# Three fixed experts in place of two, in a mixture-of-experts stage that streams its weights

## Chip, cores and metric

The kernel runs on one core of one Trainium2 chip. The metric is the device time of one execution in microseconds (us). Three runs of the kernel before gave 758.07, 760.01 and 759.18 us, median 759.18 us.

## What is computed

An encoder trunk of two layers over 256 tokens of 1024 features, all in float32. Layer 0 mixes tokens by gated linear attention, layer 1 by a gated recurrence (RG-LRU). Each mixer is followed by a mixture of 16 experts. The part that matters here:

```python
N_EXPERTS, N_GROUPS, TOP_K, D_EXPERT = 16, 4, 2, 512

def grouped_moe(h, router_w, router_bias, w_gate, w_up, w_down):
    scores = jax.nn.sigmoid(t @ router_w)              # 256 tokens x 16 experts
    ...        # the best of 4 groups of 4 experts, then the best 2 experts in it
    for e in range(N_EXPERTS):
        he = jax.nn.silu(t @ w_gate[e]) * (t @ w_up[e])
        out = out + combine[:, e:e + 1] * (he @ w_down[e])

def setup_inputs(seed=0): ...
```

Each token goes to two experts, so 512 places are dealt out per layer. An expert's weights are 6 MB (gate, up and down, 2 MB each), all experts of a layer 96 MB. How many tokens an expert gets follows from the inputs alone. The reference's router, evaluated over `setup_inputs(0)` (jax with its present default random generator), gives for experts 0 to 15:

| layer | tokens per expert |
|---|---|
| 0 | 19, 32, 31, 40, 49, 25, 75, 33, 6, 7, 2, 11, 44, 13, 46, 79 |
| 1 | 27, 37, 33, 27, 24, 42, 12, 30, 13, 16, 26, 15, 73, 27, 46, 64 |

## The kernel before

All weights go through one ring of 17 tiles of 1 MB (`SLOTS`), in the order of one long list of pieces (`Stream`). SyncE's queue issues every load; `Stream.get` hands out the next piece and issues loads up to `look` pieces ahead. A tile of the ring can be loaded again when the piece, 17 allocations earlier, has been used. Some intermediate tensors (`big`) take tiles of the same ring.

The experts are computed in 7 **units** of 128 token places each (`UNITS`, L28 to L36). An entry `(kind, i, n)` gives `n` times 32 places to one expert: kind `"s"` is the fixed expert number `i`, kind `"r"` is the expert of rank `i` when the other experts are sorted by their token counts, largest first. So in the kernel before experts 0 and 1 are fixed with 64 places each, ranks 0 and 1 of the other fourteen have 96 places each, ranks 2 to 7 have 64, and ranks 8 to 13 have 32. `NS` is the number of fixed experts, `ND = 16 - NS` that of the sorted ones.

`route_order` (L934) works out the sorting on VectorE at the end of the routing, just before the expert stage; SyncE reads an expert's number from its result (`value_load`, L242) before the first load of a sorted expert, as the load's address depends on it. A fixed expert's load has no such wait (`f.known`, L257). `Stream.ahead` stops at the first piece that is not known yet. In `out_route` (L499) and again in `gather_end` (L928), after `route_order`, the stream is told to go 16 pieces ahead; the first unit's 12 pieces are those of the fixed experts. Each unit gathers its tokens, multiplies by gate and up (`up_proj`, L1023, called twice), applies silu and product on ScalarE and VectorE, transposes, multiplies by down, and adds the weighted result into `x` (`scatter`, L1056).

`route_end` (L955) compares each expert's token count with its places (`ce`, 32 times `n`) and sets a flag if any count is larger (L972 to L975). `overflow` (L1063), which is called ahead of the sixth unit in both layers (L1137), reads the flag on the engines and skips its body when it is 0. When it is 1, the body computes, for the tokens that found no place, all 16 experts over all 256 tokens, one expert per turn of a hardware loop:

```python
with tc.If(flag > 0):                      # L1067
    ...
    with tc.For_i(0, NE, 1) as e:          # L1079
        def load(name, n, j, q):
            t = h.rearrange("p m n -> p (m n)")
            nc.sync.dma_start(t, I[name][l][ds(e, 1), q * n:(q + 1) * n, :] ...)
```

Each `load` brings 1 MB into the same tile `h`; there are six per turn (gate, up and down, two halves each), and after each one there are eight 128x512 matmuls that read it (two blocks of 128 tokens times four). Between up and down lie silu, a product, eight transposes and two copies; after the second half of down, four times a `scalar_tensor_tensor` and a `tensor_add` of 128x512 on VectorE.

Of the kernel before, what the change touches and what calls it, by code (L numbers as in the profile page):

```python
# [26 lines left out]

UNITS = [  # L28
    [("s", 0, 2), ("s", 1, 2)],
    [("r", 0, 3), ("r", 8, 1)],  # L30
    [("r", 1, 3), ("r", 9, 1)],
    [("r", 2, 2), ("r", 3, 2)],
    [("r", 4, 2), ("r", 5, 2)],
    [("r", 6, 2), ("r", 7, 2)],
    [("r", 10, 1), ("r", 11, 1), ("r", 12, 1), ("r", 13, 1)],
]  # L36
NS = 2
ND = NE - NS
SLOTS = 17
HALVES = [slice(0, 512), slice(512, 1024)]  # L40
# [35 lines left out]
def trunk(ctx, tc, I, out):  # L76
# [8 lines left out]
    stream = Stream(ring, SLOTS - 4)  # L85

    def bank():
        return pp.tile([P, 512], F32, name="ps")
# [66 lines left out]
    for u, unit in enumerate(UNITS):  # L155
        at = 0
        for kind, i, n in unit:
# [6 lines left out]
            at += n  # L164
    G.iota(rtab[:, 2, :], pattern=[[1, ND]], base=NS, channel_multiplier=0, allow_small_or_imprecise_dtypes=True)

# [58 lines left out]
    def part(t, a, q):  # L225
        sl, at = TAIL[q]
        nc.sync.dma_start(t[:, at:at + 4 * (sl.stop - sl.start)].rearrange("p (j n) -> p j n", j=4),  # L227
                          a[:, :, sl].rearrange("o (p j) n -> (o p) j n", j=4))

    def moe_piece(l, name, kind, i, s, last):  # L230
        src = I[name][l]
        n, j = (512, 4) if name != "moe_w_down" else (256, 2)
        last = last and name == "moe_w_down"

        def f(t):
            if kind == "s":
                assert not last
                a = src[i, s * n:(s + 1) * n, :].rearrange("(p j) n -> p (j n)", j=j)
            else:
                if (l, i) not in regs:  # L240
                    with tc.issue_after(mark["load"]):
                        regs[l, i] = nc.sync.value_load(order[l][0:1, i:i + 1], min_val=NS, max_val=NE - 1)  # L242
                a = src[ds(regs[l, i], 1)]
                if last:

                    late.append((t, a))
                    part(t, a, s)
                    if len(late) == 2 * len(UNITS[-1]):
                        for q in range(2, len(TAIL)):
                            for t, a in late[len(UNITS[-1]):]:  # L250
                                part(t, a, q)
                        late.clear()
                    return
                a = a[:, s * n:(s + 1) * n, :].rearrange("o (p j) n -> (o p) (j n)", j=j)
            b = nc.sync.dma_start(t, a)  # L255
            mark["load"] = b.ins
        f.known = lambda: kind == "s" or order[l] is not None  # L257
        return f

    def moe_pieces(l, unit):  # L260
        return [moe_piece(l, name, kind, i, s, unit is UNITS[-1]) for name in ("moe_w_gate", "moe_w_up", "moe_w_down")
                for s in range(2) for kind, i, n in unit]

# [2 lines left out]
    def plan(l, text):  # L266

        for n in text.split():
            if n[0] == "a":
                stream.add("a", *ada_pieces(l, int(n[1]), int(n[2])))  # L270
            elif n[0] == "A":
                stream.add("a", *ada_pieces(1, int(n[1]), int(n[2])))
            elif n[0] == "i":
                w = (gw_in, lw_in)[l]
                stream.add("i", k_piece(w, 0, int(n[1]) * 512), k_piece(w, 1, int(n[1]) * 512))
            elif n[0] in "IJ":
                stream.add("i", k_piece((gw_in, lw_in)[l], "IJ".index(n[0]), int(n[1]) * 512))
            elif n == "r":
                stream.add("r", gate_piece(I["lru_w_r"][0]), gate_piece(I["lru_w_i"][0]))
            elif n == "o":  # L280
                stream.add("o", *[row_piece(I[("gla_w_out", "lru_w_out")[l]][0], q) for q in range(4)])
            else:
                stream.add("u", *moe_pieces(l, UNITS[int(n[1])]))
# [111 lines left out]
    def rsqrt2(ss):  # L395

        r = sm.tile([P, NM], F32, name="rstd2", bufs=1)
        b = V.scalar_tensor_tensor(r, ss[:, 0], EPS, ss[:, 1], op0=OP.add, op1=OP.add)  # L398
        mark["rsqrt"] = b.ins
        G.tensor_tensor(r, r, half[:, 0:NM], op=OP.pow)  # L400
        return [r[:, m:m + 1] for m in range(NM)]
# [472 lines left out]
    def slots(R, tab, name, ms, first=False):  # L874


        n = len(ms)
        m0 = ms[0]
        pos = R["ps"][:, m0 * NE:(m0 + n) * NE].rearrange("p (m e) -> p m e", m=n)
        ov, sl = rt("ov" + name, n, NE), rt("sl2", NM, NE)[:, 0:n]  # L880
        pw, sv, su = rt("pw2", NM, 2, NE)[:, 0:n], rt("sv" + name, n * 2), rt("su" + name, n * 2, 4)
        V.tensor_tensor(ov, pos, tab[:, 1, None, :].to_broadcast([P, n, NE]), op=OP.is_ge)
        V.tensor_tensor(sl, pos, tab[:, 0, None, :].to_broadcast([P, n, NE]), op=OP.add)
        V.scalar_tensor_tensor(sl, ov, FAR, sl, op0=OP.mult, op1=OP.add)
        V.tensor_tensor(pw, R["oh"][:, m0:m0 + n], sl[:, :, None, :].to_broadcast([P, n, 2, NE]), op=OP.mult)
        V.tensor_reduce(sv, pw.rearrange("p m c e -> p (m c) e"), axis=AX.X, op=OP.add)
        if first:
            return ov, sv, sv[:, :, None]
        V.tensor_tensor(su, sv[:, :, None].to_broadcast([P, 2 * n, 4]), utab[:, None, :].to_broadcast([P, 2 * n, 4]),
                        op=OP.subtract)  # L890
        return ov, sv, su
# [42 lines left out]
    def route_order(l, R):  # L934
# [5 lines left out]
        cmp, prod = [tmp[:, i * 256:i * 256 + ND * ND].rearrange("p (e r) -> p e r", e=ND) for i in range(2)]  # L940
        V.scalar_tensor_tensor(key, cnt[:, NS:], 16.0, desc[:, NS:], op0=OP.mult, op1=OP.add)
        V.tensor_tensor(cmp, key[:, None, :].to_broadcast([P, ND, ND]), key[:, :, None].to_broadcast([P, ND, ND]),
# [12 lines left out]
    def route_end(R, cnt, cmp, prod):  # L955

        for i, dst in ((0, be), (1, ce)):
            V.tensor_mul(prod, cmp, rtab[:, i, None, :].to_broadcast([P, ND, ND]))
            V.tensor_reduce(dst[:, NS:], prod, axis=AX.X, op=OP.add)
        ov, sv, su = slots(R, bc, "", [0, 1])  # L960
# [32 lines left out]
    def moe(l, h, hT, R, gs, g2, done=None):  # L993
# [18 lines left out]
        def groups(unit):  # L1012

            w = min(n for _, _, n in unit)
            w = {1: 1, 2: 2, 4: 4}[w]
            res, at = [], 0
            for i, (_, _, n) in enumerate(unit):
                for q in range(0, n, w):
                    res.append((i, (at + q) * 32, w * 32))
                at += n  # L1020
            return res

        def up_proj(unit, xg, t0):  # L1023
            ps = bank()
            for s in range(2):
                w = [stream.get("u").rearrange("p (j n) -> p j n", j=4) for _ in unit]
                for j in range(4):
                    k = 4 * s + j
                    for i, p0, n in groups(unit):
                        T.matmul(ps[p0:p0 + n], xg[:, k, t0 + p0:t0 + p0 + n], w[i][:, j, :], start=k == 0, stop=k == 7)  # L1030
            return ps
# [99 lines left out]
        for u, unit in enumerate(UNITS):  # L1131
            y = mid("y")
            t0 = (u - 1) % 2 * P if u else 0
            if u == len(UNITS) - 2:
                scatter(*pend)
                pend = None
                overflow()  # L1137
            pg = up_proj(unit, xg, t0)
            if u:
                settle()  # L1140
            pu = up_proj(unit, xg, t0)
            if u == 0:
                spread(R)
# [11 lines left out]
            j = 4 if last else 2  # L1155
# [7 lines left out]
            if last:  # L1163
                for q, (sl, _) in enumerate(TAIL):
                    if q < 2:
                        w = [stream.get("u") for _ in unit]
# [23 lines left out]
    h, hT, R = out_route(0, oT, g1, gf, rest)  # L1190
    ss0 = sm.tile([P, 3, NM], F32, name="ss3", bufs=1)
    moe(0, h, hT, R, gf, g2, done=lambda q: last_squares(q, ss0))
    stream.look = SLOTS - 4
    h, hT = norm(rsqrt2(ss0), gn)
# [16 lines left out]
    def done(q):  # L1211
        last_squares(q, ss)
        for m in range(NM):
            sl = TAIL[q][0]
            V.tensor_mul(o[m][:, sl], x[:, m, sl], fg[0][:, sl])  # L1215

    moe(1, h, hT, R, gf, g2, done)
    r = rsqrt2(ss)
    with tc.issue_after(mark["rsqrt"]):
# [29 lines left out]
```

## Time and profile before

| what | value |
|---|---|
| median of the three runs | 759.18 us |
| the profiled execution's own time | 757.96 us |
| its span, first to last instruction | 756.2 us |
| TensorE busy | 699.6 us, 93% |
| VectorE busy | 340.4 us, 45% |
| ScalarE busy | 131.4 us, 17% |
| bytes moved, mean rate over the span | 286.27 MB, 379 GB/s |

The profile has a page with the busy time of each engine and the span in 40 slices of 18.9 us; and views of the trace: groups of instructions by line, the busy time in chosen stretches, who waited for whom, the chain of waits that ended last, the instructions in order of time, and all instructions of one line. PE is TensorE's matmuls, PEld its weight loads, DVE VectorE, ACT ScalarE, SPq SyncE's queue. A matmul that is pipelined behind another starts before that one has ended, so the time per matmul in a run of them is the busy time of the group over its count, and less than the mean duration. The granted clock is that of TensorE as a share of 2.4 GHz.

### The profile page before, as it was taken

The page shows a single profiled execution, that of the slowest core. Times are in us where ns is not written, and L with a number is a line of the kernel's source. Part 1 is how long each engine was busy: PE and PEld are TensorE (multiplying, and loading weights), DVE is VectorE, ACT ScalarE, POOL GpSimd, SP SyncE. Part 2 cuts the span into 40 slices and gives each one's busy share as a digit, 9 for nine tenths or more (in the row PEclk, how much of TensorE's full clock was granted, in tenths as well). Part 3 has the DMA queues.
Part 4 walks back from the last instruction along what each step waited for, and adds up shares of the span by engine and source line. Part 5 has one row for each costly group of instructions (what it writes and reads, how often), then busy time and mean ns, then how long its engine had stood idle before and what let it go on. Part 6 is the DMA issues. An engine that isn't in the chain of part 4 may idle for free. (4 is left out here: it accounts for less than half of the span.)

```text
span 756.2 us, 9538 instructions
## 1 busy us (share of the span) xinstructions
PE 699.6 (93%) x3559; PEld 342.8 (45%) x3559; DVE 340.4 (45%) x780; ACT 131.4 (17%) x257; POOL 27.4 (4%) x69
## 2 busy tenths in 40 slices
PE   4899899999999999999887999998999999999874
PEld 3345745454633533533226888655433433433212
DVE  3626983897413223231023589996523143140214
ACT  5006112122200000000013166123210010010002
POOL 5000001000000000000000014000000000000000
PEclk9999999999999999999999999999999999999998
DMA  9999999779999999999999999991999999999994
GB/s 304 384 386 387 386 396 386 269 318 384 423 370 422 421 421 420 423 409 422 411 363 379 381 367 350 406 377 59 423 421 419 419 421 421 421 420 410 422 373 150
DMA packets 80445, 286.27 MB, mean 379 GB/s; under 512 B 5991, under 2 KB 16280, under 8 KB 57866
## 3 DMA queue, kind: packets, MB, share of 16 engines
q1 hardware_dynamic: 78752, 284.71, 96.0%
q10 hardware_dynamic: 1258, 0.66, 0.3%
q8 instruction: 30, 0.49, 0.3%
q0 software_dynamic: 384, 0.23, 0.1%
q14 instruction: 21, 0.17, 0.1%
HBM read 284.54 MB, written 1.05 MB: 378 GB/s over the span
## 5 line engine op out<-in xcount | busy, mean ns | idle before, releaser
L1030 PE MATMUL ps<-w 128*32 128x512 f32 (+1 forms) x1280 | 204.1, 593 | 9.6 <-DMA w<-in_moe_w_up_dram 7.4
L1030 PEld LDWEIGHTS ps<-w 128*32 128x32 f32 (+1 forms) x1280 | 61.8, 121 | 148.7 <-issue 121.7
L1041 PE MATMUL ps<-w,s 128*32 128x512 f32 (+1 forms) x512 | 85.0, 594 | 2.7 <-ACT s L1160 2.7
L1147 DVE TENSOR_TENSOR s<-s,ps 128x512 f32<-128x512 f32 x14 | 9.6, 688 | 149.6 <-PE ps L1030 149.6
L1061 DVE TENSOR_TENSOR x<-x,ps 128x512 f32<-128x512 f32 (+1 forms) x60 | 39.1, 652 | 59.7 <-PE ps L1060 59.7
L317 DVE SCALAR_TENSOR_TENSOR acc<-w,cond,acc 128x512 f32<-128x512 f32 x84 | 64.8, 794 | 1.1
L473 PE MATMUL ps<-w 128*128 128x512 f32 x128 | 59.3, 599 | 0.0
L1060 PE MATMUL ps<-mid,s 128*128 128x512 f32 (+1 forms) x120 | 55.1, 581 | 2.9 <-DVE mid L1168 2.6
L740 PE MATMUL ps<-hT,w 128*128 128x256 f32 x256 | 55.7, 379 | 0.0
L1041 PEld LDWEIGHTS ps<-w,s 128*32 128x32 f32 (+1 forms) x512 | 25.6, 123 | 58.3 <-issue 50.9
L740 PEld LDWEIGHTS ps<-hT,w 128*128 128x128 f32 x256 | 48.7, 191 | 6.7 <-ACT hT L423 0.2
L1179 DVE TENSOR_TENSOR mid<-ps,gate 128x512 f32<-128x512 f32 x24 | 16.6, 692 | 64.7 <-PE ps L1041 64.7
L561 PE MATMUL ps<-w,hT 128*128 128x512 f32 x96 | 42.5, 596 | 1.8 <-DVE hT L425 1.0
L904 PE MATMUL ps<-onehot,h 128*128 128x256 f32 x192 | 42.4, 379 | 0.0
L317 DVE SCALAR_TENSOR_TENSOR gate<-w,cond,gate 128x512 f32<-128x512 f32 x56 | 40.9, 748 | 0.9
L1146 ACT ACTIVATE s<-ps 128x512 f32<-128x512 f32 x14 | 8.4, 597 | 183.6 <-PE ps L1030 183.6
L904 PEld LDWEIGHTS ps<-onehot,h 128*128 128x128 f32 x192 | 36.4, 190 | 7.0 <-issue 2.4
L1060 PEld LDWEIGHTS ps<-mid,s 128*128 128x128 f32 x120 | 20.5, 190 | 30.8 <-issue 20.1
L1160 ACT COPY s<-ps 128x512 f32<-128x512 f32 x14 | 8.2, 586 | 147.2 <-PE ps L1158 147.2
L529 PE MATMUL ps<-w,hT 128*128 128x512 f32 x64 | 29.6, 619 | 3.7 <-DVE w L637 3.7
L473 PEld LDWEIGHTS ps<-w 128*128 128x128 f32 x128 | 22.8, 191 | 20.7 <-issue 18.9
L561 PEld LDWEIGHTS ps<-w,hT 128*128 128x128 f32 x96 | 17.8, 190 | 23.9 <-issue 21.0
(261 smaller groups left out, 602.5 us busy)
## 6 DMA issues: line engine op xcount, KB each, us to landing
w<-in_moe_w_gate_dram SPq DMA_DIRECT2D x64, 1024.0 KB, 11.2
w<-in_moe_w_up_dram SPq DMA_DIRECT2D x64, 1024.0 KB, 15.7
w<-in_moe_w_down_dram SPq DMA_DIRECT2D x56, 1024.0 KB, 17.8
w<-in_ada_w_dram SPq DMA_DIRECT2D x48, 1024.0 KB, 13.5
w<-in_gla_w_in_dram SPq DMA_DIRECT2D x12, 1024.0 KB, 14.6
w<-in_moe_w_down_dram SPq DMA_DIRECT2D x16, 512.0 KB, 9.5
w<-in_lru_w_in_dram SPq DMA_DIRECT2D x8, 1024.0 KB, 12.5
w<-in_gla_w_out_dram SPq DMA_DIRECT2D x4, 1024.0 KB, 12.5
```

Of the source, the lines that this page charges most:

```text
L317: V.scalar_tensor_tensor(acc, w, cond[:, k:k + 1], acc, op0=OP.mult, op1=OP.add)
L473: T.matmul(ps, yT[:, k, m * P:(m + 1) * P], w[k // 2][:, k % 2, sl], start=k == 0, stop=k == 7)
L529: T.matmul(ps, hT[:, k, m * P:(m + 1) * P], w[k // 4][:, k % 4, :], start=k == 0, stop=k == 7)
L561: T.matmul(pst[i][m], hT[:, 4 * b + j, m * P:(m + 1) * P], w[:, j], start=b == 0 and j == 0, stop=b == 1 and j == 3)
L740: T.matmul(ps[:, 0:S], w[k // 4][:, k % 4, ct * P:(ct + 1) * P], hT[:, k, :], start=k == 0, stop=k == 7)
L904: T.matmul(ps[j // 2][:, j % 2 * 2 * P:(j % 2 + 1) * 2 * P], hv[:, b, j, :], oh, start=m == 0 and j % 2 == 0, stop=m == 1 and j % 2 == 1, ...
L1030: T.matmul(ps[p0:p0 + n], xg[:, k, t0 + p0:t0 + p0 + n], w[i][:, j, :], start=k == 0, stop=k == 7)
L1041: T.matmul(ps[hf][p0:p0 + n], aT[:, k, p0:p0 + n], w[i][:, j, hf * 512:(hf + 1) * 512], start=k == 0, stop=k == 3)
L1060: T.matmul(ps, wt[:, m * P:(m + 1) * P], y[:, sl], start=True, stop=True)
L1061: V.tensor_add(x[:, m, sl], x[:, m, sl], ps)
L1147: V.tensor_mul(act, act, pu)
L1179: V.tensor_mul(y[:, sl], py[hf], g2[:, sl])
```

## The change

Expert 2 becomes a third fixed expert, with 64 places in the second unit, beside rank 1, which has 64 places there. Rank 0 and rank 8 make the third unit. The thirteen sorted experts have 96 places (rank 0), 64 (ranks 1 to 7) and 32 (ranks 8 to 12). For the second unit the list of pieces has expert 2's four gate and up pieces first, then the other expert's four, then the down pieces in turn; `up_proj` takes the first four pieces together and holds them for its two calls.

```diff
 UNITS = [
     [("s", 0, 2), ("s", 1, 2)],
+    [("s", 2, 2), ("r", 1, 2)],
     [("r", 0, 3), ("r", 8, 1)],
-    [("r", 1, 3), ("r", 9, 1)],
     [("r", 2, 2), ("r", 3, 2)],
     [("r", 4, 2), ("r", 5, 2)],
     [("r", 6, 2), ("r", 7, 2)],
-    [("r", 10, 1), ("r", 11, 1), ("r", 12, 1), ("r", 13, 1)],
+    [("r", 9, 1), ("r", 10, 1), ("r", 11, 1), ("r", 12, 1)],
 ]
-NS = 2
+NS = 3
...
     def moe_pieces(l, unit):
+        if unit is UNITS[1]:
+
+            return [moe_piece(l, name, kind, i, s, False) for kind, i, n in unit for name in ("moe_w_gate", "moe_w_up")
+                    for s in range(2)] + [moe_piece(l, "moe_w_down", kind, i, s, False) for s in range(2) for kind, i, n in unit]
         return [moe_piece(l, name, kind, i, s, unit is UNITS[-1]) for name in ("moe_w_gate", "moe_w_up", "moe_w_down")
                 for s in range(2) for kind, i, n in unit]
...
+        held = []
+
         def up_proj(unit, xg, t0):
             ps = bank()
+            if unit is UNITS[1] and not held:
+                look, stream.look = stream.look, stream.look - 4
+                held.extend(stream.get("u") for _ in range(4))
+                stream.look = look
             for s in range(2):
-                w = [stream.get("u").rearrange("p (j n) -> p j n", j=4) for _ in unit]
+                w = [(held.pop(0) if held and i == 0 else stream.get("u")).rearrange("p (j n) -> p j n", j=4)
+                     for i in range(len(unit))]
```

## Rows read from the trace of the kernel before

**Rows 1.** The page: TensorE's share, and GB/s in 40 slices of the span

```profile
PE 699.6 (93%) x3559; PEld 342.8 (45%) x3559; DVE 340.4 (45%) x780; ACT 131.4 (17%) x257; POOL 27.4 (4%) x69
GB/s 304 384 386 387 386 396 386 269 318 384 423 370 422 421 421 420 423 409 422 411 363 379 381 367 350 406 377 59 423 421 419 419 421 421 421 420 410 422 373 150
```

**Rows 2.** Stretches (us): length, busy time of PE, PEld, DVE, ACT, POOL, clock, DMA share, GB/s

```profile
515.00:520.00 5.00, 3.74 (x19) 2.27 (x19) 3.74 (x12) 1.61 (x4) 0.55 (x1) 1.00 0.01 3
...
525.00:530.00 5.00, 5.00 (x30) 2.86 (x30) 3.43 (x12) 2.79 (x7) 0.00 (x0) 1.00 0.28 79
530.00:535.00 5.00, 5.00 (x26) 1.64 (x24) 4.83 (x28) 1.19 (x1) 0.00 (x0) 1.00 1.01 423
160.00:170.00 10.00, 9.99 (x52) 5.13 (x50) 9.09 (x34) 2.40 (x6) 0.17 (x1) 1.00 0.90 370
170.00:180.00 10.00, 8.19 (x64) 5.67 (x64) 7.33 (x37) 2.47 (x4) 0.40 (x1) 1.00 0.92 378
```

**Rows 3.** Waits of SyncE's queue, first of 150:185, then of 500:530 (total, times, longest)

```profile
SPq L242 <- DVE r_ordi L951: 10.1, 1, 10.1
...
SPq L242 <- DVE r_ordi L951: 17.6, 1, 17.6
```

**Rows 4.** All instructions of L1067 in 315:345 (the skipped branch, layer 0), three rows

```profile
L1067 PEldq COMPARE_BRANCH  x1: 352/352/352, 328.9 to 328.9; - x1
L1067 DVEq EVENT_SEMAPHORE  x1: 21/21/21, 332.2 to 332.2; - x1
  PE ps L1030: 1.3, 1
```

**Rows 5.** TensorE in order of time around that branch (start, us, what)

```profile
327.19 3.70 PE L1060 MATMUL ps<-mid,s 128*128 128x512 f32 x8
332.23 13.95 PE L1030 MATMUL ps<-w 128*64 128x512 f32 x64 [1.33 <-DVEq L1067]
```

**Rows 6.** SyncE's queue in order of time, unit 0 and later, layer 1

```profile
527.42 2.69 SPq L255 DMA_DIRECT2D w<-in_moe_w_gate_dram  x4
531.83 4.34 SPq L255 DMA_DIRECT2D w<-in_moe_w_up_dram  x4
```

**Rows 7.** Groups by line and shape: count, busy us, mean ns, idle before

```profile
L473 PE MATMUL ps<-w 128*128 128x512 f32 x128 | 59.3, 599 | 0.0
...
L317 DVE SCALAR_TENSOR_TENSOR gate<-w,cond,gate 128x512 f32<-128x512 f32 x56 | 40.9, 748 | 0.9
...
L476 DVE TENSOR_TENSOR x<-x,s 128x512 f32<-128x512 f32 x8 | 5.5, 689 | 0.1
```

**Rows 8.** DMA issue to landing: x (512 KB each, L104), then L255 in 527:529

```profile
DMA to landing us min/median/max: 3.7/4.2/4.8
...
L255 SPq DMA_DIRECT2D w<-in_moe_w_gate_dram x2: 343/346/348, 527.4 to 528.6; - x2
...
DMA to landing us min/median/max: 6.1/6.1/6.1
```

**Rows 9.** Chain that ended last: a matmul's end and the load that it let start

```profile
677.10 14.00 PE ps L1030 x64
691.65 19.83 DMA w<-in_moe_w_up_dram
...
715.14 1.07 PE ps L1060 x2
717.40 15.24 DMA w<-in_moe_w_down_dram
```

**Rows 10.** Stretches with a fall of TensorE's clock (columns as in rows 2)

```profile
91.00:94.00 3.00, 0.09 (x2) 0.00 (x0) 2.55 (x17) 0.00 (x0) 0.00 (x0) 1.00 1.05 386
...
95.00:97.00 2.00, 2.00 (x3) 0.97 (x4) 2.00 (x7) 0.00 (x0) 0.00 (x0) 0.50 1.05 387
...
733.00:736.00 3.00, 3.00 (x16) 0.64 (x12) 0.00 (x0) 0.00 (x0) 0.00 (x0) 0.50 1.10 349
736.00:737.00 1.00, 1.00 (x13) 0.33 (x6) 0.00 (x0) 0.00 (x0) 0.00 (x0) 0.91 1.17 362
```

## The prediction made before the change was run

> **What bounds the kernel now.** I read the rate of the DMA engines over the span first, then the stretches where it falls, then who waits there. The reader is to see two things in the 40 slices [rows 1]: the stream runs at about 420 GB/s through both expert stages, and falls to 59 GB/s in one slice, with smaller dips in layer 0. The stretches show that slice from near: from 515 to 529 us nothing moves [rows 2]. SyncE's waits name the reason: for 17.6 us it waits for the expert order, the last product of the routing, before it may load the first sorted expert; in layer 0 it waits 10.1 us, but there earlier loads are still in flight, at 370 to 378 GB/s [rows 2, 3]. TensorE is busy 93% [rows 1], so the two are near balance, and what the stream gains here is paid out only where TensorE later waits for weights.
>
> **What the change saves.** Expert 2's four gate and up pieces need no order. In layer 1 they can be loaded inside the hole: one piece of 1.05 MB at 423 GB/s is 2.48 us, four are 9.9 us [rows 2]. Not all of it stays. Before, the order's arrival let four pieces go at once, at 527.4 us, and the fifth at 531.8, when unit 0's first pieces had been used [rows 6]. After the change those four tiles are filled already, so the first sorted piece goes at 531.8 too, 4.4 us later than now. Net 9.9 - 4.4 = 5.5 us, between 0 (TensorE takes over as the bound) and 9.9. In layer 0 the dips are shallow: 0.12 and 0.10 of two 10 us stretches below 421 GB/s, 2.2 us [rows 2]; I take 2, between 0 and 4. Sum: -7.5 us.
>
> **What it adds beside that.** `held` keeps two up pieces in the ring while gate runs, so tiles come free half a unit later, once per layer; a pause in SyncE's issuing there is covered by the pieces already queued ahead of it. That unit's matmuls become pairs of 64 columns, as unit 0's, in place of fours of 32; the bytes stay, and so do the pieces. The sort shrinks from 14 to 13. All of these I cost at nothing; without the queued pieces, the pause would be up to one gate phase, half of the 13.95 us that a unit's gate and up take [rows 5].
>
> **The places.** The step that decides comes from the reference, not from the trace. Rank 1 had 96 places and gets 64. In layer 0 the largest counts are 79 (expert 15) and 75 (expert 6), neither of them fixed. So rank 1 is expert 6, with 75 tokens: 75 <= 96 before, 75 > 64 after. `route_end` sets the flag and `overflow` runs its body in layer 0, all 16 experts over all tokens, for 11 places. The nearest decision between two groups there has a margin of 0.001 in the scores, so rounding does not move 11 tokens. In layer 1 rank 0 has 73 (<= 96) and rank 1 exactly 64, which is not more than 64; ranks 2 to 7 have at most 46 and rank 8 has 24: no flag there. In the trace of before the branch is skipped [rows 4, 5], as it should be with 79 and 75 places under 96.
>
> **What a turn of that loop costs.** The trace of before does not show one, so each part goes by the nearest rows.
> - Wait for a load. All six loads of a turn go into one tile, so none starts before the last matmul on the one before has ended. From that end to the issue: 691.10 to 691.65, 0.55 us, and 716.21 to 717.40, 1.2 us [rows 9]; I take 0.6, the simpler load. From issue to landing with nothing in front: 3.7 us for 512 KB [rows 8], and 1.24 more for the other half at 423 GB/s, 4.9. The other row agrees: of two pieces issued at 527.4 and 528.6 the second landed 6.1 after its issue, so one alone at about 4.8 [rows 8]. Together 5.5 us, between 5.35 and 7.3 (1.2 + 6.1).
> - Matmuls. Eight at 59.3 / 128 = 0.46 us [rows 7] are 3.7 us at the high clock, 7.4 at half. After an idle stretch of 3 us the clock was at 0.50 although matmuls ran densely, in one place for over 2 us, in another through 733 to 736 and most of the way to 737 [rows 10]. Here every burst follows 5.5 idle us. I take 3.5 us at half clock, which does 1.75 us of the work, and 1.95 us at full: 5.45 us.
> - One piece 10.95 us, six 65.7. Silu, product and transposes lie inside the wait for the first down piece.
> - End of a turn. VectorE's four pairs take 4 x (0.75 + 0.69) = 5.8 us [rows 7]; they can start after two of the last eight matmuls, 1.85 us into the burst, so 2.2 us stick out.
> - Jump back. The nearest row is the skipped branch, for which TensorE stood 1.3 us [rows 4, 5]. I take 1.5, between 0.6 and 4.
> - Sum 65.7 + 2.2 + 1.5 = 69.4 us; 16 turns 1110 us. Way in and out (16 transposes, as many small copies, a few small operations) 8 us.
>
> The loads that are queued when the loop begins hold up its first load, and give the same time back afterwards, as they need not be waited for: zero.
>
> The Trainium skill (Runtime: NRT & Kernel Launch, Instruction fetch mechanics) says that a taken branch whose target isn't in the window already fetched must wait for that code; by it, the jumps would cost a fetch each, and no row here prices one inside a loop. The skipped branch is such a jump, over a long body, and the trace gives it 1.3 us; by the page the sum could only rise.
>
> **The sum.** Against the profiled execution: 757.96 - 7.5 + 1110 + 8 = 1868 us. That execution is 1.2 us under the median of 759.18, nothing beside this.
>
> **The rivals.**
> - *The flag stays 0, and the kernel is faster.* The mechanism is the filled hole alone: 757.96 - 7.5 = 750 us, from 745 to 757. It decides as soon as rank 1 has at most 64 tokens in both layers, which needs other inputs than the ones I counted; with jax's older random generator the two largest counts of layer 0 would be 65 and 52. For it: the hole of 14 us is real [rows 2]. Against: the reference's own seed is 0, and 75 is far from 64.
> - *The clock stays low through the loop.* 6 x (5.5 + 7.4) + 1.4 + 1.5 = 80.3 us a turn, 757.96 - 7.5 + 1285 + 8 = 2043 us. For it: half of each turn is idle. Against: it came back within about 4 us of dense work wherever it fell [rows 10]. The Trainium skill (TensorE: Matmul & The Clock Gate, HAM oscillation) tells of a kernel in which each wait for a load put the whole next burst into the slow clock; by that this rival would be the forecast, but its bursts were shorter than these, and the rows here show the return.
> - *The clock stays high.* 6 x (5.5 + 3.7) + 3.0 + 1.5 = 59.7 us a turn, 1714 us. Against: each wait is longer than the idle stretch that lowered it [rows 10].
> - *Layer 1 overflows too.* If one more token goes to its rank 1, 65 > 64, the loop runs twice: 1868 + 1118 = 2986 us. The nearest second-against-third choice there has a margin of 0.0002, so rounding is unlikely to do it.
>
> **How the numbers follow.** Forecast 0.55, low clock 0.15, high clock 0.10, flag stays 0 0.13, both layers 0.03, something else 0.04. The predicted time is 1868 us. The range runs from the high clock less the lower ends of wait and jump (1714 - 14 - 14, and some 45 for an end of turn that is hidden) to the low clock with 40 for the jump and half of the wait's upper end (2043 + 40 + 86): 1640 to 2160, which leaves out about 0.2. About 0.3%, 2.3 us, is what a measurement can tell from no change: slower 0.87; of the flag's 0.13, faster 0.11 and within that bound 0.02.
>
> **What would show it.** Right: in the trace after, 768 more matmuls of 128x512 (48 a turn) in one stretch that starts near 330 us and takes some 1100, all at the lines of `overflow`; six 1 MB loads per turn, each some 11 us after the one before; a DMA rate of about 91 GB/s there (six pieces, 6.3 MB, in 69 us); the clock falling in each wait; and no such stretch in layer 1. The hole at 515 to 529 us of before, now some 1100 us later, is shorter by about 10 us. Wrong: no matmul at these lines. If they are there and a turn is far from 69 us, the wait for a load and the clock are the terms to look at.

## The result, and the profile after

The changed kernel takes 2124.76 us (2121.73 to 2126.46, three runs) against 759.18 before: 2.798 times as long, 95% interval 2.792 to 2.804. The flag is set in layer 0, the slow path runs there once, and the steps of the prediction's argument can be looked up in the trace.

From the page of the changed kernel: TensorE's busy time, the granted clock in tenths and the rate in 40 slices, now of 53 us each.

```profile
PE 1573.5 (74%) x5047; PEld 710.5 (33%) x5047; DVE 461.1 (22%) x971; ACT 171.9 (8%) x327; POOL 27.4 (1%) x71
...
PEclk9999998888888888888888888888888899999999
...
GB/s 356 387 323 388 418 421 209 59 79 79 79 59 79 79 69 69 79 79 72 66 79 79 59 79 79 72 68 78 79 76 62 79 352 373 366 325 389 421 414 311
```

[Rows 1] showed one hole in the rate. Here the rate lies at 59 to 79 GB/s from the eighth slice to the thirty-second: 25 slices, some 1330 us, in layer 0. The clock is down in these slices and in the one before them, in which the loop begins. Layer 1 has no such stretch.

Groups of instructions by line (count, busy us, mean ns, idle before and what ended it): the matmuls of the slow path, and VectorE's operations at the end of its turns.

```profile
L1107 PE MATMUL ps<-h,hT 128*128 128x512 f32 x1024 | 571.8, 722 | 358.2 <-DMA h<-in_moe_w_gate_dram 203.2 <-DMA h<-in_moe_w_up_dram 155.1
L1129 PE MATMUL ps<-h,mid 128*128 128x512 f32 x512 | 282.1, 714 | 130.4 <-DMA h<-in_moe_w_down_dram 130.4
...
L1135 DVE SCALAR_TENSOR_TENSOR mid<-ps,o_cc,gate 128x512 f32<-128x512 f32 x64 | 48.0, 751 | 355.1 <-PE ps L1129 355.1
...
L1136 DVE TENSOR_TENSOR x<-x,mid 128x512 f32<-128x512 f32 x64 | 44.3, 692 | 2.2
```

Two things are to be seen. TensorE stands 358.2 + 130.4 = 488.6 us until one of 96 loads has landed, 5.1 us each. And there are 1024 + 512 = 1536 matmuls of 128x512, 16 for each load, where the prediction had counted 768: in float32 each matmul of the code is two instructions in this trace.

The place of [rows 5] in the changed kernel, TensorE in order of time (two stretches): the last work ahead of the flag, the first of the slow path, and the sixth unit behind it.

```profile
327.77 3.70 PE L1071 MATMUL ps<-mid,s 128*128 128x512 f32 x8
331.30 1.91 PE L437 MATMUL ps<-ident,h 128*128 128x128 f32 x16
...
1703.51 13.95 PE L1041 MATMUL ps<-w 128*64 128x512 f32 x64 [2.08 <-DVE x L1136]
```

The sixth unit starts at 1703.51 in place of 332.23, 1371.3 us later, and that is the whole of the loss: the spans differ by 2123.0 - 756.2 = 1366.8.

One turn of the loop in order of time (start, us, engine, line, what), from the last burst of the turn before.

```profile
668.36 8.83 PE L1129 MATMUL ps<-h,mid 128*128 128x512 f32 x16 [4.77 <-DMA h<-in_moe_w_down_dram]
...
678.01 0.69 DVE L1136 TENSOR_TENSOR x<-x,mid 128x512 f32<-128x512 f32 x1
680.05 0.17 DVE L1098 COPY o_cc<-o_co 128x2 f32 x1 [1.35 <-PEq L1090]
680.08 14.46 SPq L1093 DMA_DIRECT2D h<-in_moe_w_gate_dram  x2
684.95 9.22 PE L1107 MATMUL ps<-h,hT 128*128 128x512 f32 x16 [7.77 <-DMA h<-in_moe_w_gate_dram]
698.98 8.83 PE L1107 MATMUL ps<-h,hT 128*128 128x512 f32 x16 [4.81 <-DMA h<-in_moe_w_gate_dram]
...
712.59 8.83 PE L1107 MATMUL ps<-h,hT 128*128 128x512 f32 x16 [4.78 <-DMA h<-in_moe_w_up_dram]
726.24 8.83 PE L1107 MATMUL ps<-h,hT 128*128 128x512 f32 x16 [4.82 <-DMA h<-in_moe_w_up_dram]
...
739.95 8.80 PE L1129 MATMUL ps<-h,mid 128*128 128x512 f32 x16 [3.28 <-DMA h<-in_moe_w_down_dram]
753.58 8.83 PE L1129 MATMUL ps<-h,mid 128*128 128x512 f32 x16 [4.83 <-DMA h<-in_moe_w_down_dram]
```

Burst, wait, burst, wait: each load is issued when the burst before it has ended, and each burst begins when its load has landed. The next turn's first load is issued at 765.30, so a turn is 765.30 - 680.08 = 85.2 us, and 16 turns are 1363.5.

From issue to landing of the six loads of a turn (L1093), first over all 96, then for the loop's first load alone, which is issued at 333.2 us while the stream's queued loads still move 421 GB/s (333 to 336 us):

```profile
DMA to landing us min/median/max: 4.7/4.8/8.4
...
DMA to landing us min/median/max: 8.4/8.4/8.4
```

The stretches inside two bursts (length, busy PE, PEld, DVE, ACT, POOL, clock, DMA share, GB/s), which answer to [rows 10]:

```profile
685.00:688.00 3.00, 3.00 (x4) 1.44 (x5) 0.00 (x0) 0.00 (x0) 0.00 (x0) 0.50 0.00 0
688.00:689.00 1.00, 1.00 (x2) 0.34 (x1) 0.00 (x0) 0.00 (x0) 0.00 (x0) 0.50 0.00 0
689.00:694.00 5.00, 5.00 (x12) 1.90 (x10) 0.00 (x0) 0.00 (x0) 0.00 (x0) 0.98 0.00 0
694.00:699.00 5.00, 0.19 (x2) 0.02 (x1) 0.00 (x0) 0.00 (x0) 0.00 (x0) 1.00 0.59 210
699.00:699.50 0.50, 0.50 (x1) 0.28 (x2) 0.00 (x0) 0.00 (x0) 0.00 (x0) 0.95 0.00 0
699.50:702.50 3.00, 3.00 (x5) 1.33 (x4) 0.00 (x0) 0.00 (x0) 0.00 (x0) 0.50 0.00 0
...
703.00:708.00 5.00, 4.81 (x12) 1.83 (x10) 0.00 (x0) 0.75 (x2) 0.00 (x0) 1.00 0.00 0
```

Each burst runs for a while at half clock, although its matmuls follow each other without a gap, and then at full: in the first, four matmuls start in 3 us at 0.50, twelve in 5 us at 0.98. The first burst of a turn, behind 7.77 idle us, is at half clock from its start. The second, behind 4.81, is not: the granted clock is 1.00 all through the wait (694 to 699) and falls only some 0.5 us after the burst has begun. It is low for 3.4 us then. The other four bursts of the turn show the same.

### The profile page after: what moved, and what is told of

Read it like the earlier page. It is cut to its first block, busy times and chain, and to the rows that moved or that the text cites. A ratio compares the mean times of both kernels' runs of the same rounds, so it can differ in the third digit from the quotient of the medians.

```text
span 2123.0 us, 14216 instructions
## 1 busy us (share of the span) xinstructions
PE 1573.5 (74%) x5047; PEld 710.5 (33%) x5047; DVE 461.1 (22%) x971; ACT 171.9 (8%) x327; POOL 27.4 (1%) x71
## 5 line engine op out<-in xcount | busy, mean ns | idle before, releaser
L1107 PE MATMUL ps<-h,hT 128*128 128x512 f32 x1024 | 571.8, 722 | 358.2 <-DMA h<-in_moe_w_gate_dram 203.2
L1107 PEld LDWEIGHTS ps<-h,hT 128*128 128x128 f32 x1024 | 230.8, 231 | 698.7 <-issue 426.7
L1129 PE MATMUL ps<-h,mid 128*128 128x512 f32 x512 | 282.1, 714 | 130.4 <-DMA h<-in_moe_w_down_dram 130.4
L1129 PEld LDWEIGHTS ps<-h,mid 128*128 128x128 f32 x512 | 113.6, 227 | 288.7 <-issue 198.3
L1041 PE MATMUL ps<-w 128*64 128x512 f32 (+1 forms) x1152 | 203.7, 600 | 7.7 <-DMA w<-in_moe_w_up_dram 4.8
L1135 DVE SCALAR_TENSOR_TENSOR mid<-ps,o_cc,gate 128x512 f32<-128x512 f32 x64 | 48.0, 751 | 355.1 <-PE ps L1129 355.1
L1041 PEld LDWEIGHTS ps<-w 128*64 128x64 f32 (+1 forms) x1152 | 63.6, 126 | 144.5 <-issue 123.2
L1052 PE MATMUL ps<-w,s 128*64 128x512 f32 (+1 forms) x448 | 85.0, 595 | 2.7 <-ACT s L1171 2.7
L1136 DVE TENSOR_TENSOR x<-x,mid 128x512 f32<-128x512 f32 x64 | 44.3, 692 | 2.2
L565 PE MATMUL ps<-w,hT 128*128 128x512 f32 x96 | 42.5, 596 | 1.9 <-DVE hT L429 1.0
```

Of the source, the lines that this page charges most:

```text
L565: T.matmul(pst[i][m], hT[:, 4 * b + j, m * P:(m + 1) * P], w[:, j], start=b == 0 and j == 0, stop=b == 1 and j == 3)
L1052: T.matmul(ps[hf][p0:p0 + n], aT[:, k, p0:p0 + n], w[i][:, j, hf * 512:(hf + 1) * 512], start=k == 0, stop=k == 3)
L1107: T.matmul(pm[m], hT[:, k, m * P:(m + 1) * P], w[:, j], start=k == 0, stop=k == 7)
L1129: T.matmul(py[m][hf], aTs[m][:, k], w[:, j, hf * 512:(hf + 1) * 512], start=k == 0, stop=k == 3)
L1135: V.scalar_tensor_tensor(tmp, py[m][hf], cc[:, m:m + 1], g2[:, sl], op0=OP.mult, op1=OP.mult)
L1136: V.tensor_add(x[:, m, sl], x[:, m, sl], tmp)
```

## The experiments

**The places alone, in the kernel before.** Two fixed experts, the old order of the stream, rank 1 with 64 places:

```diff
-    [("r", 1, 3), ("r", 9, 1)],
+    [("r", 1, 2), ("r", 9, 2)],
```

> The kernel before with two fixed experts and its own order of the stream; only rank 1's places go from 96 to 64 (rank 9 gets the 32). Theory (the places set the flag in layer 0, 75 > 64): the loop of 16 turns runs, some 85 us each, 759 + 1367 = about 2125 us, within 10. Rival (the time comes from the third fixed expert or the new order of its pieces): no loop, 759 us.

Measured: 2124.92 us, the changed kernel's time, with the same 1024 and 512 matmuls in the slow path. The loss is in the places. The third fixed expert and the order of its pieces have no part in it.

**The change with places enough.** Ranks 0 and 1 keep 96 places each:

```diff
-    [("s", 2, 2), ("r", 1, 2)],
-    [("r", 0, 3), ("r", 8, 1)],
-    [("r", 2, 2), ("r", 3, 2)],
-    [("r", 4, 2), ("r", 5, 2)],
-    [("r", 6, 2), ("r", 7, 2)],
+    [("s", 2, 2), ("r", 2, 2)],
+    [("r", 0, 3), ("r", 7, 1)],
+    [("r", 1, 3), ("r", 8, 1)],
+    [("r", 3, 2), ("r", 4, 2)],
+    [("r", 5, 2), ("r", 6, 2)],
```

> The changed kernel with its third fixed expert and its order of pieces, but ranks 0 and 1 with 96 places each, ranks 2 to 6 with 64 and ranks 7 to 12 with 32, so that 79, 75 and 73, 64 fit. Theory: no loop in either layer, and the early load of expert 2's pieces is all that is left. By the trace of the changed kernel, where the expert stage of layer 1 ended 1.8 us nearer to its start than before and layer 0 no earlier up to the flag: 755 to 758 us. By the prediction's own term for it: 751 us. Rival (the loss is in the order of the pieces): over 762 us.

Measured: 757.99 us beside 759.65 of the kernel before on that chip, ratio 0.9976 (0.9966 to 0.9987). Run again later: 758.16 beside 759.05, 0.9979 (0.9966 to 0.9991). No loop, and a gain of 0.2%, within the 0.3% that the prediction set as a bound; not the 7.5 us of the prediction's term.

**Half the turns.** `For_i(0, NE, 1)` becomes `For_i(0, 8, 1)` in the changed kernel.

> The changed kernel with 8 turns of the loop in place of 16, so experts 8 to 15 are left out of the slow path (part of the computation is left out). Theory (the time is the number of turns times 85.2 us, way in and out near zero): 2124.8 - 8 x 85.2 = 1443 us. Rival (a large fixed cost of the branch or of its code): clearly more than 1443 us.

Measured: 1442.32 us. Eight turns are 682.4 us, 85.3 each; nothing is left for a large fixed cost of the branch.

**Half the matmuls per load.** In the loop of the changed kernel `for m in range(NM)` becomes `for m in range(1)` for both groups of matmuls, and the second block of 128 tokens shares the first block's matmul results. So its tokens get the expert outputs of other tokens.

> The changed kernel with the loop's matmuls for one block of 128 tokens in place of two, so the second block of the slow path is not computed (part of the computation is left out): 8 matmul instructions read each load in place of 16; loads, VectorE and ScalarE as they are. Theory (the prediction's matmul term was half of what it is, as each matmul of the code is two instructions in float32): a burst of 8 x 0.43 + 1.75 for the half clock at its start = 5.2 us, a turn 6 x (4.8 + 5.2) + 2.9 = 62.9 us, 2124.8 - 16 x 22.3 = 1768 us. Rival 1 (shorter bursts stay at half clock to their end): 6.9 us a burst, a turn 73 us, 1930 us. Rival 2 (the length of a burst does not hang on the number of matmuls): 2125 us.

Measured: 2943.31 us, which none of the three foresaw. The loop runs in both layers here. The second block's wrong values change layer 0's output for the 11 tokens without a place (they all lie in that block), and so layer 1's counts: the reference's router, given layer 0's output with this error, sends 66 tokens to expert 15 in place of 64. That is over the limit. Per turn the run still answers. In order of time, around the end of one turn:

```profile
667.14 5.40 PE L1129 MATMUL ps<-h,mid 128*128 128x512 f32 x8 [4.80 <-DMA h<-in_moe_w_down_dram]
...
677.71 11.56 SPq L1093 DMA_DIRECT2D h<-in_moe_w_gate_dram  x2
682.57 6.33 PE L1107 MATMUL ps<-h,hT 128*128 128x512 f32 x8 [10.03 <-DMA h<-in_moe_w_gate_dram]
```

Eight instructions take 5.40 us in most bursts, against 5.2 expected and 8.83 for sixteen; the wait stays at 4.8 to 5.0. So the length of a burst hangs on the number of instructions, and the clock comes back inside this shorter burst too (at half clock to its end it would be 6.9, as the first rival had it). A turn is (2943.3 - 758) / 32 = 68.3 us, not 62.9. Some 2.3 us of that are VectorE's eight operations, which now outlast the burst: from the last burst's end at 672.5 to the next load at 677.7 it is 5.2 us in place of 2.9. Another 2.6 are the bursts, as the first two of a turn take 6.33 and 5.86 us.

**Loads beside matmuls.** The six loads of a turn go in turn into `h` and one tile of the ring:

```diff
+                two, turn = [h.rearrange("p m n -> p (m n)"), big("two")], []
...
-                        t = h.rearrange("p m n -> p (m n)")
+                        t = two[len(turn) % 2]
+                        turn.append(q)
```

> The changed kernel with the loop's six loads going in turn into two tiles, so a load runs while the matmuls of the one before run. Theory (each turn holds six waits of 4.8 us for a load, and each of them costs 1.75 us more by the clock at the start of the burst behind it): one wait and one fall of the clock a turn are left, 4.8 + 6 x 6.9 + 1.75 + 1.5 for the step between up and down + 2.9 = 52.3 us a turn, 2124.8 - 16 x 32.9 = 1598 us, and a clock near 1.0 in most of the loop. Rival (the loads are not what the loop waits for, or the clock stays low): above 1800 us.

Measured: 1604.16 us, and a turn of 52.3 us by its loads. In order of time:

```profile
659.11 8.59 PE L1109 MATMUL ps<-h,hT 128*128 128x512 f32 x16 [7.81 <-DMA h<-in_moe_w_gate_dram]
667.53 7.03 PE L1109 MATMUL ps<-w,hT 128*128 128x512 f32 x16
...
674.40 7.03 PE L1109 MATMUL ps<-h,hT 128*128 128x512 f32 x16
```

Only the first burst of a turn waits for a load and runs slow at first; the others find theirs landed and take 7.03 us, sixteen instructions 0.43 us apart. Five waits and five falls of the clock, 5 x (4.8 + 1.8), are 33 us a turn: what the loop pays for its single tile.

**Where the gain of the early load goes.** First a miss:

> As e2_places96, but expert 2's pieces wait for the order as a sorted expert's do, so nothing is loaded early; its place in the units and in the list of pieces stays. If the early load is worth 2 to 4 us: 758 to 760 us, e2_places96 faster by that. If the gain of e2_places96 is from the shape of the units or the smaller sort: the same time as e2_places96.

Measured: 757.89 us. It tells nothing of the early load: marking expert 2's pieces as not known moved no wait into SyncE's queue, and its trace has them issued at 511 to 518 us, ahead of the order. So the next kernel makes SyncE read the order before the first of them:

```diff
+                if i == 2 and (l, 2) not in regs:
+                    with tc.issue_after(mark["load"]):
+                        regs[l, 2] = nc.sync.value_load(order[l][0:1, 2:3], min_val=NS, max_val=NE - 1)
```

> As e2_places96, but SyncE reads the expert order before it issues expert 2's first piece, so that none of its pieces is loaded early. (In e3_no_early the wait was not there: the pieces went out ahead of the order all the same, and its time is that of e2_places96.) If the early load is what makes e2_places96 1.7 us faster than the kernel before: the hole in the stream of layer 1 is back, and the time is that of the kernel before, 759.5 us, within 1. If the gain is from the shape of the units or the sort: 758 us as e2_places96.

Measured: 757.92 us, beside 758.16 of the kernel with the early load on the same chip. With or without it, the time is the same. Stretches of 10 us in layer 1 (columns as above), first with the early load:

```profile
510.00:520.00 10.00, 8.74 (x42) 5.36 (x41) 5.91 (x29) 2.71 (x7) 0.55 (x1) 1.00 0.95 400
520.00:530.00 10.00, 8.60 (x52) 5.68 (x53) 7.22 (x38) 4.23 (x9) 0.00 (x0) 1.00 0.30 122
530.00:540.00 10.00, 10.00 (x50) 3.41 (x48) 5.91 (x31) 1.83 (x2) 0.00 (x0) 1.00 0.71 276
540.00:550.00 10.00, 10.00 (x44) 6.68 (x40) 3.77 (x8) 2.30 (x4) 0.00 (x0) 1.00 1.01 423
550.00:560.00 10.00, 9.32 (x47) 3.90 (x47) 3.76 (x9) 1.05 (x2) 0.00 (x0) 1.00 0.65 251
```

and without it:

```profile
510.00:520.00 10.00, 8.74 (x45) 5.69 (x44) 5.80 (x25) 2.85 (x7) 0.55 (x1) 1.00 0.23 93
520.00:530.00 10.00, 8.61 (x49) 5.27 (x49) 7.15 (x38) 4.23 (x9) 0.00 (x0) 1.00 0.24 79
530.00:540.00 10.00, 10.00 (x48) 3.30 (x46) 5.30 (x28) 1.16 (x2) 0.00 (x0) 1.00 1.01 425
540.00:550.00 10.00, 10.00 (x44) 7.13 (x41) 4.44 (x10) 2.30 (x4) 0.00 (x0) 1.00 1.02 422
550.00:560.00 10.00, 9.32 (x46) 3.47 (x46) 3.76 (x9) 1.05 (x2) 0.00 (x0) 1.00 1.01 422
```

The hole is filled at 510 to 520; at 520 to 530 it stays, and two others open, at 530 to 540 and at 550 to 560. Over 500 to 570 us the two kernels miss nearly the same: 17.0 us of streaming at 421 GB/s with the early load, 17.8 without. SyncE's waits in 500 to 560, of the kernel with the early load, name what stands there:

```profile
SPq L255 <- PE ps L1052: 13.6, 2, 11.9
```

It waits 11.9 us for unit 0's first down matmul to free a tile. Without the early load it waits as long, and it issues the pieces behind expert 2's at nearly the same times. SyncE's queue with the early load, then without:

```profile
538.74 4.37 SPq L255 DMA_DIRECT2D w<-in_moe_w_down_dram  x4
555.79 4.72 SPq L255 DMA_DIRECT2D w<-in_moe_w_gate_dram  x4
...
538.06 4.37 SPq L258 DMA_DIRECT2D w<-in_moe_w_down_dram  x4
555.11 4.34 SPq L258 DMA_DIRECT2D w<-in_moe_w_gate_dram  x4
```

Without the early load the DMA engines have a row of pieces still to move during that wait (422 GB/s at 550 to 560). With it they run out of them (251): the ring is full, and nothing is left to load. That can be tried: let unit 0 use its down pieces sooner, by putting its gather for the next two units behind them.

```diff
-            if u % 2 == 0 and u + 1 < len(UNITS):
+            if u and u % 2 == 0 and u + 1 < len(UNITS):
                 xg = prepare(u // 2, R["su"])
...
             py = down_proj(unit, aT)
+            if u == 0:
+                xg = prepare(0, R["su"])
```

> As e2_places96, but in the first unit of each layer the gather for the next two units comes after the down matmuls in place of before them. Theory (with the early load the ring is full and the stream stands at 550 to 555 us in layer 1 until the first down pieces are used): the down pieces are used some 7 us earlier, that second hole shrinks, and up to 3 us are gained at the end: 755 to 757.5 us. Rival (the expert stage waits for the gather, or the silu chain is no longer covered): 759 us or more.

Measured: 754.0 us, ratio 0.9919 (0.9899 to 0.9939); run again, 753.53 us, 0.9922 (0.9901 to 0.9942). This is the version that beats both kernels. The same stretches:

```profile
530.00:540.00 10.00, 10.00 (x48) 3.30 (x46) 4.53 (x26) 0.60 (x1) 0.00 (x0) 1.00 0.88 340
540.00:550.00 10.00, 9.30 (x42) 3.52 (x40) 1.99 (x4) 1.66 (x3) 0.00 (x0) 1.00 1.01 421
550.00:560.00 10.00, 8.58 (x40) 6.28 (x38) 2.87 (x7) 1.26 (x3) 0.00 (x0) 1.00 1.01 423
560.00:570.00 10.00, 10.00 (x48) 3.36 (x48) 3.48 (x8) 0.92 (x2) 0.00 (x0) 1.00 0.76 305
```

The hole at 550 to 560 is gone, a smaller one comes after it, and over 500 to 570 us the stream misses 14.8 us. From 570 to 700 us it runs without a hole in all of these kernels (389 GB/s or more in every 10 us), and what is missed before that is not made up there. Whether the new order alone does it was tried twice, in the kernel before and in the kernel whose pieces wait for the order.

> The kernel before, with two fixed experts, and the first unit's gather for the next two units put after its down matmuls, as in e8_down_first. Theory (e8_down_first is faster because the early load no longer runs into a full ring; without an early load the stream is busy from 529 us on whatever the gather does): the time of the kernel before, 759, within 1 us. Rival (the order of gather and down matmuls alone is worth the 4 to 5 us): 755 us.

Measured: 758.24 us, ratio 0.9985 (0.9972 to 0.9997): a gain of about 1 us, and not the 4 to 5 of the rival.

> e8_down_first with expert 2's pieces waiting for the order, so without the early load. Theory: 758 us, as e7_wait_order; the 4 us of e8_down_first need the early load and the order of the gather together. Rival (the order alone): 754 us as e8_down_first.

Measured: 756.79 us, ratio 0.9967 (0.9955 to 0.9979), about 1 us under the 758 expected; the interval overlaps that of the same kernel with the gather first (0.9967 to 0.9999). Over 500 to 570 us its stream misses 17.9 us, 3.1 more than with the early load. With the third fixed expert the four kernels make a table, in us:

| | gather first | down first |
|---|---|---|
| pieces wait for the order | 757.9 | 756.8 |
| pieces loaded early | 758.0 to 758.2 | 753.5 to 754.0 |

The early load is worth nothing with the gather first (757.9 against 758.2 on one chip), and some 3 us with the down matmuls first (756.8 against 753.5 on another).

## Why the prediction was right, and where it was not

- **The places: right.** The flag is set in layer 0 and not in layer 1, as the counts 75 and 64 against 64 places say. The experiment on the kernel before shows that this alone costs the whole 1366 us. How near layer 1 is to its limit, the kernel with half the matmuls showed without being asked: there the limit was passed and the loop ran twice, the fourth rival's mechanism, if by another cause than rounding.
- **Matmuls of a load: the term that was off by a factor of two.** The prediction took 8 matmuls a load from the code and 0.46 us from [rows 7]: 3.7 us at full clock. But the 0.46 is the price of one instruction, and in float32 here one matmul of the code is two in the trace. The row said so: the line of L473 stands at x128, while `out_route` calls it 4 x 8 times in each of two layers, 64. So full clock is 7.0 us, and a burst 8.83 (9.22 for the first of this turn) in place of 5.45. Six bursts are 53.3 us a turn in place of 32.7: + 20.6.
- **The clock: its cost right, its place not.** A burst of 8.83 us is 7.03 (the burst without a wait, in the experiment with two tiles) and 1.80 more. 3.4 us at half clock cost about that; the prediction had chosen 3.5. It had the clock fall in each wait, though, and behind the waits of 4.8 us it falls only when the burst has run for some 0.5 us. The two places of [rows 10] are also read loosely: in the second TensorE had stood 1.99 us ahead of 732.68 and not 3, and 0.91 for 736 to 737 means a low clock for some 0.2 us of it, not most of it. The rivals with the clock low or high throughout are both out: at half clock to its end a burst would be 14 us. The Trainium skill (TensorE: Matmul & The Clock Gate, HAM oscillation) tells of a kernel in which each wait for a load lets the next burst start cold. That every burst behind a wait meets the low clock holds in this trace; that it starts there holds for the first burst of a turn alone (0.50 from 685 on, but 0.95 at 699.0 to 699.5).
- **The wait: a little less.** 4.8 us in place of 5.5. Landing took 4.7 us at least and 4.8 in the median, close to the 4.8 to 4.9 worked out from [rows 8], and the 0.6 us between the last matmul and the issue was next to nothing: 707.81 to 707.84. Six waits: - 4.0 us.
- **End of a turn and jump back: right.** 2.9 us from the last burst's end to the next load, 1.5 of VectorE and 1.4 of the jump, in place of 2.2 and 1.5: - 0.8. The jump costs what the skipped branch of [rows 4, 5] did.
- **The turn.** 69.4 + 20.6 - 4.0 - 0.8 = 85.2, as measured; 16 turns are 253 us more than forecast. The forecast of 1868 and these make 2121.
- **The rest of the sum.** Ahead of the flag the changed kernel is 0.6 us behind, where the prediction had 2 us of gain for layer 0. Way in and out of the loop: 1371.3 - 0.6 - 1363.5 = 7.2 us, 8 forecast. In these 7.2 lie 3.6 us by which the loop's first load was held up: it landed 8.4 us after its issue in place of 4.8. From there to the end of layer 0 the kernel gains 3.3 us. The prediction had said of the loads queued at the loop that they hold up its first load and give the time back, and the two numbers fit that, though no run separates them from other causes. To the flag of layer 1 it loses 0.7 again, and from there to the end it gains 1.8.
- **The early load: mechanism right, gain wrong.** The pieces do go into the hole of [rows 2], as the row of 510 to 520 shows. The step that failed is 9.9 - 4.4 = 5.5: it followed the first sorted piece only, and not the ring after it. The stream, once ahead, runs into a full ring, and stands until unit 0's down matmuls free tiles. The prediction's lower end, 0, was given to TensorE as the new bound; it was the ring.
- **The range held by luck.** With the same allowances for jump and wait the forecast itself would reach to 1868 + 40 + 86 = 1994 us. The range reached 2160 only because of the low clock's 2043 (and its sum is 2043 + 40 + 86 = 2169). The low clock did not come, the jump cost 1.4 us and the wait less than forecast. That 2125 lies near 2043 is chance: a rival's burst of 7.4 us, too few matmuls at half clock throughout, lies nearer to the measured 8.83, twice as many mostly at full, than the forecast's 5.45 does.

Open is the gain of 1.1 us that the third fixed expert shows even where its pieces wait for the order (0.9983, 0.9967 to 0.9999). It is not the early load, it is near the noise, and what it is was not tried.

## What to carry to other kernels

Where a kernel has a slow path for data that don't fit, work out from the inputs whether a change of sizes sends it there before any row of a trace is read: one expert's count over its limit cost 1366 us here, where the early load was worth some 3 at best. Price a matmul of the code by how many instructions the trace shows for such a call, not by the row's time per instruction alone. And a transfer that is started earlier gains only as far as there is a free tile to go on into: look at what frees the tiles next.

## What the runs showed of the hardware

- In float32 a 128x512 matmul of the code is two instructions in the trace (1024 and 512 for 512 and 256 calls), 0.43 us each at the full clock; sixteen of them take 7.03 us.
- A load of 1 MB with nothing in front of it takes 4.7 to 4.8 us from issue to landing (least and median of 96), so a loop that loads, waits and computes moves six pieces in 85.2 us, 74 GB/s, where the stream moves 421.
- A wait of 4.8 us costs TensorE more than its own length: the burst behind it is 1.80 us longer, as 3.4 us of it run at half clock. The granted clock still reads 1.00 at the end of such a wait and falls some 0.5 us into the burst. Overlapping the loads took both costs away for five of the six, 33 us of 85.2.
